# A hybrid decoder step in float32: v and h turned by transposing DMAs instead of TensorE, with h's norm moved into the sigmoid and the weights

## The chip, the cores and the metric

The kernel runs on one core of one Trainium2 chip. The metric is the device time of one execution in microseconds (us). The engines are TensorE (PE in the profile; PEld is its loading of weights), VectorE (DVE), ScalarE (ACT), GpSimd (POOL) and SyncE (SP, which here only queues DMAs). SBUF is the on-chip memory of 128 partitions, PSUM the accumulator memory that PE writes.

## The reference

One layer, 1024 prompt tokens and 8 sample tokens, model width 1024, everything float32. Cut to what matters here:

```
xn = rmsnorm(h, pre_g);  u, v, z_a, x_b, z_b, g_a, g_b = split(xn @ w_in)        # 7 x 1024 columns
vn = layernorm(gelu(v), ln_g, ln_b)                                             # over the 1024 channels of a token
y_a = gelu(u) * (tril(w_s[g]) @ vn + b_s[g]) * silu(z_a)                        # within chunks of 128 tokens, 8 groups
y_b = (pooled(x_b) @ w_pool) * scale * silu(z_b)
m = sigmoid(g_a) * (y_a @ w_pa) + sigmoid(g_b) * (y_b @ w_pb)
h = h + rmsnorm(m @ w_out, post_g)
e = p @ w_ple
gate = sigmoid(rmsnorm(h, ple_in_g) @ w_pg)
h = h + rmsnorm(gate * e, ple_out_g)
```

Outputs are h of both token sets, the normalised v of the last chunk and of the sample, and the pooling buffers.

## The kernel before

**Products.** Every float32 matrix is cut into a high and a low part (`split`: ACT rounds the high part, DVE subtracts it), and a product is three matmuls, high x high, high x low, low x high. The matrices are multiplied by Strassen's scheme with 7 products in place of 8 (`strassen`): a pair of 256 output columns takes 7 steps of 12 or 24 matmuls. A step is named here by the part of the moving operand that it streams: B11, T2, B21, T3, T4, T1, B22, with `x` in front in the profile for the input, `ya`, `yb`, `wo`, `wg` later. Its stationary parts are `vw`, `gaw`, `mw`, `hw` and so on. `evacuate` takes the sums out of PSUM, by ACT for the first product (`u`), mostly by DVE else. PSUM holds three accumulators (`acc`, `acct`) and two small banks.

**Stages, in order of time.** x is normalised and turned (to about 50 us); then v (four pairs, the first without Strassen), g_a, u and z_a, x_b and z_b, g_b, the two merging products, the output product m @ w_out (from about 825 us) and the gate product (to 993 us). Activations lie channels by tokens up to the merge; `big` is one tile of 128 x 8 x 1032 words that holds in turn x, v by tokens, the merged m and the normalised h.

**v.** The v products leave channels by tokens (`v`, one tile for 128 channels), but the layer norm and the mixing need tokens by channels. `v_turn` transposes 128 x 128 blocks on PE into a bank (`vt`), and ACT reads the bank, applies gelu and writes `big`, with the sum of a row as a by-product (`vsums`). The turns of a pair hang on the steps of the next. After the last pair `ln_stats`, `ln_apply`, `v_split` and `spatial` (matmuls `mix`) follow tile by tile in the g_a stage; for the eight sample tokens the same is done in `sv`, and their mixing is the small matmul group `smix`.

**h.** After a pair of 128-token tiles of the output product, `out_finish` normalises it and a DMA queued by POOL adds x. `gate_norm` squares h (ACT), takes the root (POOL, `rstd`) and multiplies (DVE, `hn`); `gate_input` transposes hn on PE into banks (`pht`), and ACT copies these into `big`, times the gain ple_in_g, which is by then one number for each partition. The gate product takes them as `hw`.

**w_pg.** `column_sums` loads w_pg in the x_b and z_b stages (`wgraw`), forms the Strassen sums and stores them in DRAM; the parts B11 and B21 are read from w_pg itself later.

**Order.** Nobody writes the order by hand. `Planner` records every instruction, knows what each reads and writes, estimates its duration, gives it a due time (`late`, and `at` on PE's clock) and then simulates the engines: at each moment it takes, on each engine, the instruction that can start soonest, with ties by due time. The result is a fixed order for each in-order engine. SBUF has 46 slots of equal size (`SLOTS`); an instruction that first writes a slot (`o.fresh`) needs a free one, and a load must leave `SPARE` = 3 free. In the profile all recorded instructions carry the line of `play`, L293, so tiles are told by their names.

Of the kernel before, what the change touches and what calls it, by code (L numbers as in the profile page):

```python
# [10 lines left out]
BF16 = mybir.dt.bfloat16  # L11
AF = mybir.ActivationFunctionType
ALU = mybir.AluOpType

P = 128
# [39 lines left out]
class Planner:  # L55
# [25 lines left out]
    def space(self, ap):  # L81

        dims, start = list(ap.ap), ap.offset
        if "DRAM" in str(ap.space):
            row = ap.tensor.shape[-1]
            first, start = divmod(start, row)
            rows = sum(s // row * (n - 1) for s, n in dims if s >= row)
            return (ap.tensor.name, first, first + rows + 1,
                    ((start, start + sum(s * (n - 1) for s, n in dims if s < row) + 1),))
        row, parts = dims[0]  # L90
        first, start = divmod(start, row)
        pieces = [(start, start + 1)]
# [35 lines left out]
    def duration(self, engine, method, out, reads, kwargs):  # L128
        n = out.free_size()
        if engine == "tensor":  # L130
            return 0.109 if method == "transpose" else max(0.06, 0.0062 + n / 2268)
        if engine == "vector":
            if method == "tensor_reduce":
                n = reads[0].free_size()
            quick = method in ("tensor_scalar", "tensor_scalar_mul", "tensor_copy")
            quick = quick and self.tags.get(reads[0].tensor.name) in (None, "slot")
            return 0.065 + n * (0.00059 if quick else 0.00105) + (0.06 if method[:8] == "scalar_t" else 0)
        if engine == "scalar":
            return max(0.09 + n * 0.00086, 0.26 if n > 1 else 0) + (0.2 if kwargs.get("accum_out") is not None else 0)
        return 0.1 + n * 0.0008 if method == "memset" else 1.0  # L140

    def take(self, engine, method, args, kwargs):
# [14 lines left out]
        if method == "dma_start":  # L157
# [40 lines left out]
    def order(self):  # L198
# [15 lines left out]

        def soonest(o):
            t = max(free[o.engine], o.ready)
            if not o.fixed:
                lead = self.LOAD if o.moved and o.fresh else self.LEAD
                t = max(t, min(o.late - lead, o.at) + slip)
# [14 lines left out]
        while done < len(self.ops):  # L234
            best = None
            for e in self.ENGINES:
# [4 lines left out]
                if could:  # L241
# [7 lines left out]
                    if best is None or now < best[0]:  # L249
                        best = now, o  # L250
            if best is None:
# [48 lines left out]
def hybrid_step(  # L300
# [82 lines left out]
    def root(part, n=P):  # L383

        t, r = sm("ms"), sm("rstd")
# [470 lines left out]
    S = NB  # L856
    xop = Operand("x")
# [7 lines left out]

    def v_turn(out, pair, ts):

        if ts == [S]:
# [3 lines left out]
            places = [(S, ps[:NS, : 2 * P], NS)]  # L872
        else:
# [4 lines left out]
            places = [(t, ps[:, i], P) for i, t in enumerate(ts)]  # L878
        for t, src, n in places:
            nc.scalar.activation(out=vtok(t)[:n, 2 * pair * P : (2 * pair + 2) * P], in_=src,  # L880
                                 func=AF.Gelu_apprx_tanh, accum_out=vsums[:n, t, pair : pair + 1])

    class V(User):
        turns = [[0, 1], [2, 3], [4, 5], [6, 7], [S]]
# [113 lines left out]
    wgcut = {what: dram.tile([HALF, D], F32, tag="wg" + what, name="wg" + what) for what in ('T4', 'B22')}  # L998
    kept["h"] = dram.tile([T, D], F32, tag="h", name="h")
# [262 lines left out]
    for i, u in enumerate(vusers):  # L1262

        nxt = vsteps[1][3:] if i == 0 else (vsteps[i + 1][1:] if i + 1 < NPAIR else gasteps[0][0:])
        if i == 0:
            nxt = vsteps[1][2:]
# [55 lines left out]
    rows = lambda t: NS if t == S else P  # L1322
# [4 lines left out]
    def column_sums(key, src, b):  # L1327
# [25 lines left out]
    column_steps("wg", w_pg, [(bflow[9 + 7 * i], bflow[12 + 7 * i]) for i in range(4)])  # L1353
# [12 lines left out]
    h_of, parts, hn_of, samples = {}, {}, {}, {}  # L1366
# [36 lines left out]

    def gate_norm(t):

        r = rows(t)
        h = h_of.pop(t)
        hn = hn_of[t] = slot("hn", (P, D))
        rs = rstd([square_sum(h[:r], r, scratch=hn)], r)
        nc.vector.tensor_scalar_mul(hn[:r], h[:r], rs[:r])  # L1410

    def gate_input(t):

        hn = hn_of.pop(t)
        if t == S:
            samples["h"] = sample_stationary(hn, NB, gvec[:, 2 * NB :])
# [90 lines left out]
    woop, wgop = stored("wo", w_out, HALF), stored("wg", w_pg, HALF, split=wgcut)  # L1507
# [205 lines left out]
```

## Time and profile before

| | |
|---|---|
| time of 3 runs | 1001.86 us median (1001.23 to 1002.62) |
| the profiled execution | span 1002.0 us from its first to its last instruction, mean granted clock 0.996 |
| busy | PE 989.1, DVE 800.1, ACT 490.0, POOL 73.7 us |
| transposes of v on PE (`vt`) | 64 of 128 x 128 and 8 small ones, from 79.3 to 149.5 us |
| transposes of h on PE (`pht`) | 64, from 858.3 to 935.5 us |
| HBM traffic | 114.59 MB read, 51.77 MB written |

There is no time of the profiled execution beside its span; the span is 0.14 us above the median of the runs. In the rows, `out<-in` names the tile written and the tiles read, `xN` is a count, and a bracket at the end of a row is the idle time of the engine before it and what ended that. A row that gives three durations has the least, the median and the most.

### The profile page before, as it was taken

To read this page: it belongs to the slowest core of one execution; us is meant where nothing else is said; L and a number is where in the kernel's file an instruction comes from. 1 tells how busy PE (TensorE), PEld (TensorE's weight loads), DVE (VectorE), ACT (ScalarE), POOL (GpSimd) and SP (SyncE) were. 2 spreads that over 40 slices of the span, in tenths; PEclk is the share of its full clock that TensorE was granted. 3 is DMA by queue.
4 is the path that set the end of the run, shared out by engine and by line. 5 is a ranking of instruction groups with operands and counts; after the bars stand their busy time and mean duration, and the time that the engine had idled before them with its cause. 6 is when DMAs were issued, how large, how long until landed. Compare 5 with 4: busy or idle time off the path is not lost.

```text
span 1002.0 us, 16159 instructions
## 1 busy us (share of the span) xinstructions
PE 989.1 (99%) x6200; PEld 889.8 (89%) x6200; DVE 800.1 (80%) x1241; ACT 490.0 (49%) x891; POOL 73.7 (7%) x162
## 2 busy tenths in 40 slices
PE   8999999999999999999999999999999999999996
PEld 7889999999999999999999999999999988888885
DVE  5985448877788788788898887697799798779796
ACT  7664356556434343233433343552353365677653
POOL 2200001000000000000000100000000002312111
PEclk9999999999999999999999999999999999999998
DMA  9231214222364345637544166884573553389546
GB/s 353 117 121 43 84 43 129 85 85 86 101 235 169 127 167 183 210 127 252 200 158 143 61 222 244 266 305 148 199 268 107 177 201 71 80 275 364 160 109 188
DMA packets 87330, 166.95 MB, mean 167 GB/s; under 512 B 7614, under 2 KB 47598, under 8 KB 87245
## 3 DMA queue, kind: packets, MB, share of 16 engines
q1 hardware_dynamic: 84885, 158.01, 45.3%
q0 software_dynamic: 2048, 7.37, 4.3%
q8 instruction: 49, 0.80, 0.3%
q10 hardware_dynamic: 320, 0.54, 0.2%
q14 instruction: 28, 0.23, 0.1%
HBM read 114.59 MB, written 51.77 MB: 166 GB/s over the span
## 4 chain that ended last, share of the span: by engine, by line
PE 97%; DVE 1%; POOL 0%; issue 0%; ACT 0%; POOLq 0%; DVEq 0%
PE acc L293 71%; PE acct L293 15%; PE accm L293 2%; PE e L293 2%; PE sps L293 2%; PE mix L293 1%; PE vt L293 1%; PE pst L293 1%; PE pht L293 1%; PE warm L293 1%; DVE sv L293 0%; DVE ge L293 0%; PE smix L293 0%; PE state L293 0%; DVE welo L293 0%
## 5 line engine op out<-in xcount | busy, mean ns | idle before, releaser
L293 DVE TENSOR_TENSOR u<-acc,u 128x520 f32<-128x520 f32 (+1 forms) x90 | 62.5, 695 | 36.5 <-PE acc L293 35.0
L293 POOL TENSOR_TENSOR rstd<-ms,mhalf 128x1 f32<-128x1 f32 (+1 forms) x45 | 38.2, 851 | 204.8 <-DVE ms L293 182.5
L293 POOL MEMSET u<- 128x8 f32 x35 | 3.5, 105 | 556.1 <-PE acc L293 242.5
L293 ACT ACTIVATE u<-acc 128x512 f32<-128x512 f32 x39 | 23.2, 596 | 33.4 <-PE acc L293 33.1
L293 ACT ACTIVATE paw<-pas 128x512 fp32r<-128x512 f32 x16 | 10.0, 627 | 30.0 <-DVE pas L293 24.8
L293 ACT ACTIVATE pbw<-pbs 128x512 fp32r<-128x512 f32 x16 | 10.0, 629 | 29.1 <-DVE pbs L293 25.9
L293 DVE TENSOR_TENSOR big<-big 128x1024 f32<-128x1024 f32 (+4 forms) x20 | 23.6, 1215 | 0.0
L293 ACT ACTIVATE big<-vt 128x256 f32<-128x256 f32 x32 | 11.9, 380 | 21.4 <-PE vt L293 21.4
L293 ACT ACTIVATE big<-pht,gvec 128x128 f32<-128x128 f32 x64 | 18.0, 381 | 8.0 <-PE pht L293 8.0
L293 ACT ACTIVATE big<-mix 128x256 f32<-128x256 f32 x32 | 12.1, 383 | 19.0 <-PE mix L293 18.6
L293 PE MATMUL accm<-qh,wpoolw 128*128 128x260 f32 (+1 forms) x96 | 21.0, 320 | 0.0
L293 ACT ACT_TABLE_LOAD x13 | 16.7, 1283 | 4.6 <-PE acc L293 3.6
L293 DVE TENSOR_TENSOR v<-acc,u 128x520 f32<-128x520 f32 (+1 forms) x9 | 6.3, 697 | 14.9 <-PE acc L293 14.8
L293 DVE TENSOR_TENSOR acc<-acc,u 128x512 f32<-128x512 f32 (+1 forms) x16 | 11.1, 697 | 8.7 <-PE acc L293 8.7
L293 ACT ACTIVATE gbw<-gbs 128x512 fp32r<-128x512 f32 x16 | 10.0, 624 | 16.4 <-DVE gbs L293 13.8
L293 ACT ACTIVATE zaw<-zas 128x512 fp32r<-128x512 f32 x16 | 10.0, 628 | 14.9 <-DVE zas L293 10.6
L293 ACT ACTIVATE zbw<-zbs 128x512 fp32r<-128x512 f32 x16 | 10.1, 630 | 14.6 <-DVE zbs L293 7.3
L293 PEld LDWEIGHTS accm<-qh,wpoolw 128*128 128x128 f32 x96 | 15.5, 188 | 1.9
L293 DVE TENSOR_TENSOR big<-mix,big 128x256 f32<-128x256 f32 x32 | 13.2, 421 | 4.4 <-ACT big L293 3.5
L293 ACT ACTIVATE uw<-us 128x512 fp32r<-128x512 f32 x16 | 9.8, 627 | 13.7 <-DVE us L293 7.2
L293 ACT ACTIVATE zbw<-zbraw 128x512 fp32r<-128x512 f32 x12 | 7.5, 626 | 18.2 <-DMA zbraw<-in_w_in_dram 9.2
L293 ACT ACTIVATE gb<-gb 128x1032 f32<-128x1032 f32 (+1 forms) x8 | 6.8, 854 | 18.8 <-DVE gb L293 18.8
(687 smaller groups left out, 3629.8 us busy)
## 6 DMA issues: line engine op xcount, KB each, us to landing
ga<-ga SPq DMA_DIRECT2D x16, 516.0 KB
gb<-gb SPq DMA_DIRECT2D x16, 516.0 KB
ya<-za SPq DMA_DIRECT2D x8, 516.0 KB
yb<-zb SPq DMA_DIRECT2D x8, 516.0 KB
x<-in_x_prompt_dram SPq DMA_DIRECT2D x8, 512.0 KB
vraw<-in_w_in_dram SPq DMA_DIRECT2D x8, 512.0 KB
e<-e SPq DMA_DIRECT2D x8, 512.0 KB
garaw<-in_w_in_dram SPq DMA_DIRECT2D x8, 512.0 KB
```

The source lines that it names most:

```text
L293: getattr(getattr(self.nc, e), method)(*args, **kwargs)
```

## The change

v and h are no longer turned on PE. A float32 tile is seen as 16-bit words. POOL copies it into a slot with the first words of all its numbers ahead of the second words (`vw`, `hw` as a tile of 16-bit words; `hw` is also the name of the gate product's stationary parts). A transposing DMA on SP's queue turns the sixteen blocks of 128 x 128 words and writes them back over v or h. ACT puts the two halves of each number together again in `big` (`v_join`, and the new `gate_input`). For v, the gelu and its row sum follow as instructions of their own, in place in `big`, by `V.turns` = [7, 0, 1], [2, 3, 4], [5, 6]; the sample's columns are still transposed on PE, now in the first step after the pair.

h is turned raw. Its root goes to `vsums[:, t, :1]` and becomes the scale of the sigmoid (`gated`), so the multiplication on DVE is gone; the gain ple_in_g is multiplied into the rows of w_pg on ACT when `column_sums` loads it, and the left half of the result is stored in a new DRAM tile (`wgleft`), from which B11 and B21 are read. The square of h goes into `big` as a scratch place.

The planner gets durations for the new instructions, and a rule that holds slots back: an instruction that needs a fresh slot is passed over while its time lies more than 3 us beyond PE's, unless nothing else can go (`hard`).

```diff
@@ Planner.duration, Planner.take
-            return max(0.09 + n * 0.00086, 0.26 if n > 1 else 0) + (0.2 if kwargs.get("accum_out") is not None else 0)
+            return max(0.09 + n * (0.00101 if out.dtype == U16 else 0.00086), 0.26 if n > 1 else 0) + (0.2 if kwargs.get("accum_out") is not None else 0)
+        if method == "tensor_copy":
+            return 0.15 + n * 0.0011
...
-            op.busy, op.moved = 1.0 if engine == "gpsimd" else 0.45, writes[0].size() * 4e-6
+            op.busy, op.moved = 1.0 if engine == "gpsimd" else 0.45, writes[0].size() * (2e-6 if writes[0].dtype == U16 else 4e-6)
@@ Planner.order
+                if o.fresh and not hard and t > free["tensor"] + 3.0 and done > 300:
+                    return None
...
-                need = len(o.fresh) + (self.SPARE if o.moved else 0)
+                need = len(o.fresh) + (self.SPARE if o.moved and not hard else 0)
...
+            if best is None and not hard:
+                hard = True
+                continue
+            hard = False
@@ v
+    def v_planes(out, pair):
+        for m in range(2):
+            words, v = slot("vw", (P, 2, SEQ), U16), out[m][:, :SEQ].bitcast(U16)
+            nc.gpsimd.tensor_copy(out=words, in_=v.rearrange("p (t w) -> p w t", w=2))
+            nc.sync.dma_start_transpose(out=v.rearrange("p (k c) -> p k c", c=P),
+                                        in_=words.rearrange("p w t -> p (w t)"))
+    def v_join(out, pair, m):
+        c = 2 * (2 * pair + m) * P
+        nc.scalar.activation(out=big.bitcast(U16)[:, :, c : c + 2 * P].rearrange("p t (c w) -> p t c w", w=2),
+                             in_=out[m][:, :SEQ].bitcast(U16).rearrange("p (w t c) -> p t c w", w=2, c=P), func=AF.Copy)
...
-            ps = bank("vt").rearrange("p (t c) -> p t c", t=2)
-            for i, t in enumerate(ts):
-                for m in range(2):
-                    nc.tensor.transpose(ps[:, i, m * P : (m + 1) * P], out[m][:, t * P : (t + 1) * P], ident)
...
+            nc.scalar.activation(out=v, in_=ps[:NS, : 2 * P] if t == S else v, func=AF.Gelu_apprx_tanh,
+                                 accum_out=vsums[:n, t, pair : pair + 1])
...
-        for s, ts in zip(nxt, V.turns):
-            at(s, lambda u=u, i=i, ts=ts: v_turn(u.out, i, ts))
+        at(nxt[0], lambda u=u, i=i: v_turn(u.out, i, [S]))
+        at(nxt[0], lambda u=u, i=i: v_planes(u.out, i))
+        for m in range(2):
+            at(nxt[2 + m], lambda u=u, i=i, m=m: v_join(u.out, i, m))
+        for s, ts in zip(nxt[4:], V.turns):
+            at(s, lambda i=i, ts=ts: v_turn(None, i, ts))
...
-        s = 3 + 4 * n
+        s = 5 + 4 * n
         at(flow[s], lambda t=t: ln_stats(t))
@@ w_pg and h
+            for i, t in enumerate(raw if cuts else ()):
+                nc.scalar.activation(out=t, in_=t, func=AF.Copy, scale=col(2, 4 * i + b))
+                dma(kept["wgleft"][(4 * i + b) * P : (4 * i + b + 1) * P, :], t[:, :HALF])
...
-        hn = hn_of[t] = slot("hn", (P, D))
-        rs = rstd([square_sum(h[:r], r, scratch=hn)], r)
-        nc.vector.tensor_scalar_mul(hn[:r], h[:r], rs[:r])
+        nc.scalar.activation(out=spare, in_=src, func=AF.Square, scale=D ** -0.5, accum_out=n[:r])
+        root(n, r, rin(t))
+        words = slot("hw", (P, 2, D), U16)
+        nc.gpsimd.tensor_copy(out=words, in_=h.bitcast(U16).rearrange("p (c w) -> p w c", w=2))
+        h_of[t] = h.bitcast(U16).rearrange("p (k t) -> p k t", t=P)
+        nc.sync.dma_start_transpose(out=h_of[t], in_=words.rearrange("p w c -> p (w c)"))
...
-        for k4 in range(0, NB, 4):
-            ps = bank("pht")
-            for k in range(4):
-                nc.tensor.transpose(ps[:, k * P : (k + 1) * P], hn[:, (k4 + k) * P : (k4 + k + 1) * P], ident)
-            for k in range(4):
-                nc.scalar.activation(out=big[:, k4 + k, t * P : (t + 1) * P], in_=ps[:, k * P : (k + 1) * P],
-                                     func=AF.Copy, scale=col(2, k4 + k))
+        nc.scalar.activation(out=words_of(t).rearrange("p k (t w) -> p k t w", w=2),
+                             in_=got.rearrange("p (w k) t -> p k t w", w=2), func=AF.Copy)
...
-        nc.scalar.activation(out=g, in_=src, func=AF.Sigmoid)
+        nc.scalar.activation(out=g, in_=src, func=AF.Sigmoid, scale=rin(t))
```

What this does to the order is seen in three places. First ACT at the end of v, in the first steps of g_a. `vt` are the banks with the last pair's transposes, `sv` the sample's v, `gaw` weight parts, `ga<-acc` an evacuation of g_a, `vh` the squares of the layer norm and the high part for the mixing. Before:

```order
L293 ACTIVATE big,vsums<-vt_359 128x256 x2
L293 ACTIVATE gaw_369<-gas_352 128x512
L293 ACTIVATE big,vsums<-vt_364 128x256 x2
L293 ACTIVATE gaw_380<-garaw_360 128x512
L293 ACT_TABLE_LOAD
L293 ACTIVATE ga_366<-acc_357 128x512
L293 ACT_TABLE_LOAD
L293 ACTIVATE big,vsums<-vt_368 128x256 x2
L293 ACTIVATE big,vsums<-vt_371 128x256 x2
L293 ACTIVATE vh_375,ssq_376<-big,npart_374 128x1024
L293 ACTIVATE sv_109,vsums<-vt_382 8x256
```

The same place after the change, where `v_341` and `v_340` are the second and the first tile of the last pair:

```order
L306 ACTIVATE u_353<-acc_352 128x512
L306 ACTIVATE big,vsums<-big 128x256 x3
L306 ACTIVATE big<-v_341 128x8x256
L306 ACTIVATE sv_109,vsums<-vt_354 8x256
L306 ACTIVATE gaw_364<-gas_348 128x512
L306 ACTIVATE vh_371,ssq_372<-sv_109,npart_370 8x1024
L306 ACTIVATE big<-v_340 128x8x256
L306 ACT_TABLE_LOAD
L306 ACTIVATE ga_362<-acc_352 128x512
L306 ACT_TABLE_LOAD
L306 ACTIVATE big,vsums<-big 128x256 x4
```

The two joins (`big<-v`) now stand ahead of the sample's gelu and of the evacuation of g_a, and the last pair's gelus come behind both.

Second, PE at `smix`. Before, with the g_a product's step B22 ahead of it and T2 behind:

```order
L293 MATMUL acc_394<-xB22l_232,gaw_369 128x260 x2
L293 MATMUL acc_394<-xB22h_231,gaw_369 128x260 x2
L293 MATMUL smix_396<-diag,sv_109 128x8 x8
L293 MATMUL acc_414<-xT2h_244,gaw_391 128x260 x2
L293 MATMUL acc_414<-xT2l_245,gaw_391 128x260 x2
```

After, `rowsum` being two matmuls for the offsets of the mixing:

```order
L306 MATMUL acc_367<-xT4l_279,gaw_359 128x512
L306 MATMUL acc_367<-xT4h_278,gaw_359 128x512
L306 MATMUL rowsum_399<-wst_290,ones_397 128x512 x2
L306 MATMUL smix_389<-diag,sv_109 128x8 x8
L306 MATMUL acc_378<-xT1h_261,gaw_361 128x260 x2
L306 MATMUL acc_378<-xT1l_262,gaw_361 128x260 x2
```

smix has moved forward by three steps, from behind B22 to between T4 and T1 of the first pair of g_a. The steps from the last pair's T1 to it are now B11 of g_a, B22 of v, then T2, B21, T3 and T4 of g_a, with the sample's two transposes between T2 and B21.

Third, SP in the gate stage, after the change, with `h_1358` and `h_1366` the tiles of the third pair:

```order
L306 DMA wgB22l_1449<-wgB_125 128x2x512
L306 DMA wgB22h_1450<-wgB_125 128x2x512
L306 DMA h<-h_1358 128x1024
L306 DMA h<-h_1366 128x1024
L306 DMA wgB22l_1451<-wgB_125 128x2x512
L306 DMA_TRANSPOSE h_1358<-hw_1397 128x16x128
L306 DMA_TRANSPOSE h_1366<-hw_1394 128x16x128
L306 DMA out_1423<-in_ple_out_g_dram 128x1024
```

Before, the store of the first of these tiles stood ahead of twelve weight loads and the other behind six of them; now both stores, and the transposes that follow them, stand behind the run of weight loads, and nothing is left between the two transposes.

More of the change, by code (lines that the diff above doesn't have):

```diff
@@ L81, in space @@
     def space(self, ap):
-        dims, start = list(ap.ap), ap.offset
+        size = 2 if ap.dtype in (BF16, U16) else 4
+        dims, start = [(s * size, n) for s, n in ap.ap], ap.offset * size
         if "DRAM" in str(ap.space):
-            row = ap.tensor.shape[-1]
+            row = ap.tensor.shape[-1] * size
             first, start = divmod(start, row)
@@ L88, in space @@
             return (ap.tensor.name, first, first + rows + 1,
-                    ((start, start + sum(s * (n - 1) for s, n in dims if s < row) + 1),))
+                    ((start, start + sum(s * (n - 1) for s, n in dims if s < row) + size),))
         row, parts = dims[0]
         first, start = divmod(start, row)
-        pieces = [(start, start + 1)]
+        pieces = [(start, start + size)]
         for s, n in reversed(dims[1:]):
@@ L218, in soonest @@
                 lead = self.LOAD if o.moved and o.fresh else self.LEAD
-                t = max(t, min(o.late - lead, o.at) + slip)
+                term = min(o.late - lead, o.at)
+                t = max(t, term + slip)
+                if o.fresh and not hard and t > free["tensor"] + 3.0 and done > 300:
+                    return None
             if o.moved and len(rings[o.engine]) >= 8:
@@ L381, in rstd, with root @@
         return r
-    def root(part, n=P):
-        t, r = sm("ms"), sm("rstd")
+    def root(part, n=P, r=None):
+        t, r = sm("ms"), sm("rstd") if r is None else r
         nc.vector.tensor_scalar(out=t[:n], in0=part[:n], scalar1=EPS, scalar2=None, op0=ALU.add)
@@ L856, in hybrid_step @@
     S = NB
+    rows = lambda t: NS if t == S else P
     xop = Operand("x")
@@ L1352, in hybrid_step @@
     bflow = [s for x, z, _ in bsteps for p in (x, z) for s in p]
-    column_steps("wg", w_pg, [(bflow[9 + 7 * i], bflow[12 + 7 * i]) for i in range(4)])
+    column_steps("wg", w_pg, [(bflow[8 + 7 * i], bflow[11 + 7 * i]) for i in range(4)])
     def sample_product(st, op):
@@ L1506, in hybrid_step @@
     FIRST = ("P1", "P7", "P6", "P2", "P4", "P5", "P3")
-    woop, wgop = stored("wo", w_out, HALF), stored("wg", w_pg, HALF, split=wgcut)
+    woop, wgop = stored("wo", w_out, HALF), stored("wg", kept["wgleft"], HALF, split=wgcut)
     outsteps = [strassen(Turned(i, "m"), woop, Out(i), Tokens, None if i else FIRST) for i in range(NPAIR)]
```

36 lines of the change are left out of this document (20 added, 16 removed).

## The prediction

> **What bounds the kernel now.** I read the page first: the busy shares, the chain of waits, and the strip of 40 slices.
>
> ```profile
> PE 989.1 (99%) x6200; PEld 889.8 (89%) x6200; DVE 800.1 (80%) x1241; ACT 490.0 (49%) x891; POOL 73.7 (7%) x162
> ACT  7664356556434343233433343552353365677653
> PE 97%; DVE 1%; POOL 0%; issue 0%; ACT 0%; POOLq 0%; DVEq 0%
> ```
>
> PE is the chain: 97% of the span belongs to it, and it is idle for 1002.0 - 989.1 = 12.9 us in all. The list of waits says that between start and tail nothing but one wait of 0.2 us stops it:
>
> ```profile
> PE warm L293 <- POOL ident masks.py:199: 1.9, 1, 1.9
> PE e L293 <- ACT wehi L293: 1.2, 1, 1.2
> PE e L293 <- DVE welo L293: 0.8, 1, 0.8
> PE smix L293 <- DVE sv L293: 0.2, 1, 0.2
> ```
>
> So an instruction taken off PE shortens the run by what it occupies there, and an addition elsewhere costs something only when PE comes to wait for it. Next I read the busy time by stretch, the v stage first and then the output and gate stages (columns: width, PE, PEld, DVE, ACT, POOL, granted clock, DMA share, GB/s).
>
> ```profile
> 75.00:100.00 25.00, 25.00 (x177) 22.99 (x176) 14.51 (x24) 12.06 (x38) 0.00 (x0) 1.00 0.14 43
> 100.00:125.00 25.00, 25.00 (x176) 23.25 (x175) 11.91 (x18) 9.81 (x33) 0.00 (x0) 1.00 0.25 85
> 900.00:925.00 25.00, 25.00 (x119) 20.52 (x117) 22.96 (x33) 18.55 (x43) 5.36 (x5) 1.00 1.05 364
> 950.00:975.00 25.00, 25.00 (x110) 20.27 (x109) 24.03 (x41) 13.68 (x30) 4.05 (x5) 1.00 0.44 105
> sum 125.00, PE 125.00 PEld 102.12 DVE 103.48 ACT 85.66 POOL 27.38; mean PE 25.00 PEld 20.42 DVE 20.70 ACT 17.13 POOL 5.48
> ```
>
> The last row sums 850 to 975. In the v stage DVE and ACT are half idle; in the gate stage DVE has 125 - 103.5 = 21.5 us to spare in 125, and as little as 1 to 2 us in two of the stretches.
>
> **What leaves PE.** The view by tile counts the transposes; three rows of the timeline give their price.
>
> ```profile
> L293 PE MATMUL vt<-ident,v x72: 270/272/329, 79.3 to 149.5; 128*128 128x128 f32 x64, 128*8 128x128 f32 x8
> L293 PE MATMUL pht<-ident,hn x64: 270/272/299, 858.3 to 935.5; 128*128 128x128 f32 x64
> 861.95 0.39 PE L293 MATMUL acct<-woB22h,mw 128*128 128x512 f32 x1
> 864.72 1.03 PE L293 MATMUL pht<-ident,hn 128*128 128x128 f32 x8
> 865.51 0.48 PE L293 MATMUL acct<-woT2h,mw 128*128 128x512 f32 x1
> ```
>
> The 272 ns are the latency of one, not what it occupies: eight of them start at 864.72 and the next product at 865.51, so one takes 0.79 / 8 = 0.099 us. The eight transposes of the sample's v stay. 64 + 64 go: 128 x 0.099 = 12.6 us. A step of twelve products runs from 861.95 to 864.72, 2.77 us; I use it below as PE's clock.
>
> **What comes in their place.** Each of 16 blocks (8 of v, 8 of h) now passes POOL (a copy of 128 x 2048 words), SP (one transposing DMA of 512 KB) and ACT (a join of 128 x 2048 words). No row shows such an operation, so each is bounded.
>
> ```profile
> L293 POOL TENSOR_SCALAR_AFFINE_SELECT ws<-ws 128x1024 f32<-128x1024 f32 x1 | 1.7, 1725 | 25.4 <-DMA ws<-in_w_s_dram 25.4
> L293 POOL MEMSET mst<- 128x1024 f32 x1 | 1.0, 955 | 31.1 <-PE acc L293 31.1
> L293 ACT ACTIVATE hn<-h x8: 1043/1060/1102, 847.0 to 930.6; 128x1024 f32<-128x1024 f32 x8
> L293 DVE TENSOR_SCALAR hn<-h,rstd x8: 733/747/755, 850.8 to 933.8; 128x1024 f32<-128x1024 f32 x8
> 858.93 2.18 ACT L293 ACTIVATE big<-pht,gvec 128x128 f32<-128x128 f32 x8 [0.32 <-PE pht L293]
> DMA to landing us min/median/max: 5.5/6.3/10.0
> q1 hardware_dynamic: 84885, 158.01, 45.3%
> L293 SPq DMA_DIRECT2D wgraw<-in_w_pg_dram x8: 404/495/1109, 421.4 to 494.5; - x8
> ```
>
> POOL copy: by elements, twice the memset or twice the select, 1.9 to 3.45 us; I take the middle, 2.7, since a copy reads as the select does but tests nothing. Join on ACT: 1.06 us by bytes, 2.1 by elements; I take 2.1, the row being one element per lane and step. Transposing DMA: 512 KB at the 364 GB/s of the busiest stretch would be 1.4 us; the 512 KB transfers that POOL queues (x added to h, h to the result) land in 5.5 to 10.0, the row above; cut into rows of 128 words, 256 bytes, it is 2048 pieces, and a piece of q1 takes 0.453 x 16 x 1002 / 84885 = 85.6 ns of one engine, so 2048 x 85.6 / 16 = 11.0 us on sixteen. I take 5.5: nearest in size, and the lowest of its row because nothing is added here and POOL writes no descriptors. The Trainium skill, page "DMA: Bandwidth & Descriptors", section "Latency and other measured facts", has 261 GB/s for a transposing DMA with a strided middle dimension; an estimate from that is 2.0 us, by which the wait worked out next would vanish and the sum be 989.4. No run here shows it yet.
>
> In v, ACT keeps its gelus and gains eight joins, 8 x 2.1 = 17 us spread over some 70 of which it was half idle. In the gate stage it loses 8 x 2.18 = 17.4 us of copies out of PSUM and gains 8 x 2.1 = 16.8: nothing. DVE loses eight normalisations, 8 x 0.747 = 6.0 us, and the sample's. The scaling of w_pg's rows is eight ACT instructions of 1.06 us and eight stores, from 421 us, the first load, to some 20 us past the last at 494.5, where ACT's strip stands at 2 to 4 tenths; that idle time hides them, and without it they would cost 8.5 us. The root as the sigmoid's scale adds no instruction. Slots held back alter the order in which loads are queued, on SP above all; where PE's order changes outside the two stages it is two exchanges of neighbouring steps, for which I put nothing.
>
> **Where the longer path shows.** Behind a join on ACT, in order, stand weight splits and evacuations, and in one place the sample's last gelu. PE's only wait hung there already:
>
> ```profile
> 149.79 0.37 ACT L293 ACTIVATE sv<-vt 8x256 f32<-8x256 f32 x1 [0.81 <-PE vt L293]
> 158.42 1.92 PE L293 MATMUL smix<-diag,sv 8*128 8x8 f32 x16 [0.15 <-DVE sv L293]
> 160.00:165.00 5.00, 5.00 (x29) 4.94 (x29) 2.73 (x6) 2.21 (x3) 1.47 (x1) 0.66 0.87 313
> ```
>
> From that gelu to smix is 8.6 us. In the changed order the sample's gelu stands behind the join of the last pair's second tile. That tile is complete when step T1 of the last pair is evacuated (1.0 us with hand-over), then copy 2.7, DMA 5.5, join 2.1, and 8.6 to smix: 19.9 us. PE meanwhile runs B11, B22, T2, B21, T3 and T4, two sample transposes and two row sums: 6 x 2.77 + 0.2 + 0.5 = 17.3. It waits 2.6, where it waited 0.15: +2.4. With the DMA at 1.4 the chain is 15.8 and nothing waits; at 10.0 it is 24.4 and 7.1 wait. The granted clock fell to 0.66 for 5 us behind the thin work at smix, which loses 5 x 0.34 = 1.7 us; it may vanish or come twice, so +/-1.7, and 0 in the sum. The mixing of the tiles begins six steps after smix and has some 3 us of air by the same count.
>
> **Sum.** The span of the profiled execution is 1002.0, 0.1 above the median of the runs: 1002.0 - 12.6 + 2.4 = **991.8 us**. Its own range: 1002.0 - 12.6 - 0.15 - 1.7 = 987.5 to 1002.0 - 12.6 + 7.0 + 1.7 = 998.1.
>
> **Rivals.** *The transposes land late and ACT is held* (slower). At 11.0 us, the last pair costs 25.4 - 17.3 = 8.1, and 1.7 for the clock. In each of the seven other pairs ACT meets the first join four steps (11.1 us) after the tile is complete and the data at 1.0 + 2.7 + 11.0 = 14.7; the second lands 11.0 later, at 25.7, while ACT, after a join and three splits of 0.63 (the size of the split in the row below), stands there at 18.7: held for 7.0.
>
> ```profile
> L293 ACT ACTIVATE vw<-vraw 128x512 fp32r<-128x512 f32 x13 | 8.0, 629 | 3.5 <-PE acc L293 3.5
> ```
>
> Three accumulators let PE run two steps, 5.5, ahead; it waits 1.5 and loses 1.7 of clock, 3.2 x 7 = 22.4. In all 1002.0 - 12.6 + 32.2 = 1021.6. Between 5.5 us (a loss of 2.4) and 11.0 (32.2) the gain is eaten at 7.4 us a transpose: the point that decides. For it: the only comparable landings scatter up to 10.0, and 900 to 925 runs the DMA at a share of 1.05. Against: the v stage runs it at 0.14 to 0.25. The Trainium skill, page "VectorE: DVE Perf Modes", section "The three transpose paths", gives 1309 ns for one 128 x 128 block by DMA; sixteen in series would be 20.9 us, an estimate deep inside this rival; no run here shows whether they run in series.
>
> *POOL shuts DVE out in the gate stage* (still faster). These rows show the two engines in each other's way:
>
> ```profile
> 848.66 2.14 POOL L293 TENSOR_TENSOR rstd<-ms,mhalf 128x1 f32<-128x1 f32 x1 [3.03 <-DVE ms L293]
> 862.12 0.56 POOL L293 TENSOR_TENSOR rstd<-ms,mhalf 128x1 f32<-128x1 f32 x1 [2.73 <-DVE ms L293]
> 849.10 0.67 DVE L293 TENSOR_TENSOR mw<-big,mw 128x512 fp32r<-128x512 f32 x1
> 849.70 0.67 DVE L293 TENSOR_TENSOR ms<-ms,big 128x512 f32<-128x512 f32 x1
> ```
>
> The same instruction takes 0.56 us beside an idle DVE and 2.14 beside one that reads two tiles back to back. Turned round, eight copies of h at 3.45 block DVE for 27.6 us; it has 21.5 - 6.3 (this stage's half of PE's saving) + 6.0 = 21.2 free. The 6.4 left over reach PE: 991.8 + 6.4 = 998.2. Against: in the rows POOL is the one that waits, and at 2.7 the copies (21.6) about fit. The Trainium skill, page "SBUF — State Buffer", section "Who interferes with whom", says that a DVE instruction with two SBUF inputs and a GpSimd one that reads SBUF exclude each other for a whole instruction, whichever began first; by that rule the block on DVE is as real as the one the rows show on POOL.
>
> *The DMA moves single words.* 262,144 pieces at 85.6 / 16 ns are 1.4 ms each: over 20 ms in all. Then it would not be a block transpose at all; the destination of whole 128 x 16 x 128 blocks speaks against it.
>
> **How the numbers follow.** Runs spread over 1.4 us, so 0.2% (2 us) is about what can be told from no change. Forecast 0.53; DVE shut out 0.12; between them and late landing, within 2 us of 1001.9, 0.05; late landing 0.27; single words 0.03. Faster 0.65, same 0.05, slower 0.30. The range runs from 987, the forecast's low end, to 1016, a landing of 10.0 us on the line above, where the comparable row ends: it leaves out half of the late case, the single words and a little below, 0.18.
>
> **What would show it.** Right: vt only x8 and pht gone, PE busy near 976 us, PE's waits headed by smix with under 8 us, DMA to landing of the transposes under 7.4. Wrong: ACT waiting on v or h DMAs for more than 7 us a pair and PE on acc weights behind it; or DVE beyond 24 of 25 in the gate stage and its 0.67 us instructions stretched beside POOL copies; or copies above 3.45 us.

## The result, and the profile after

The changed kernel takes 1010.09 us in the median of 5 executions (1004.83 to 1011.20), the kernel before, beside it, 1001.86 (1001.23 to 1003.82): a ratio of 1.0069, 95% interval 1.0045 to 1.0092. It is 0.7% slower; 991.8 was forecast. The profiled execution is the shortest of the five, 1004.83 us with a span of 1003.1.

The page first: busy times, all DMA packets, SP's queue (q1) and POOL's (q0).

```profile
PE 978.6 (98%) x6072; PEld 876.5 (87%) x6072; DVE 803.3 (80%) x1231; ACT 516.8 (52%) x851; POOL 104.9 (10%) x178
DMA packets 121760, 177.41 MB, mean 177 GB/s; under 512 B 41022, under 2 KB 81006, under 8 KB 121677
q1 hardware_dynamic: 119317, 168.50, 49.9%
q0 software_dynamic: 2048, 7.37, 4.2%
```

PE does 10.5 us less than the 989.1 before (12.6 were summed), and the span is longer all the same: PE stands idle for 24.5 us instead of 12.9. q1 has 34,432 more packets, the sixteen transposing DMAs at 2048 pieces each and little else. Its share went from 45.3% of 1002.0 to 49.9% of 1003.1 us on 16 engines, 746 us more, which is 22 ns a piece.

The groups of the page and the views by tile (least, median and most nanoseconds of a row, then the time from issue to landing, of `vw` and of `hw`) give what the new steps cost; two rows of the timeline (start, duration) follow.

```profile
L306 POOL COPY vw<-v 128x2048 uint16<-128x2048 uint16 x8 | 16.6, 2076 | 62.8 <-DVE vw L306 30.8
L306 ACT ACTIVATE big<-v 128x2048 uint16<-128x2048 uint16 x8 | 17.2, 2151 | 8.5 <-DMA v<-vw 8.5
L306 ACT ACTIVATE big<-h 128x1024 f32<-128x1024 f32 (+1 forms) x16 | 25.7, 1608 | 14.8 <-DMA h<-hw 12.4
L306 SPq DMA_TRANSPOSE v<-vw x8: 1566/2483/5376, 70.4 to 133.6; - x8
DMA to landing us min/median/max: 4.4/6.6/8.9
L306 SPq DMA_TRANSPOSE h<-hw x8: 1647/2414/6046, 849.5 to 948.8; - x8
DMA to landing us min/median/max: 4.5/4.5/4.5
941.05 3.60 SPq L306 DMA_TRANSPOSE h<-hw  x1
946.76 2.17 ACT L306 ACTIVATE big<-h 128x2048 uint16<-128x2048 uint16 x1 [7.69 <-DMA h<-hw]
```

The copy (2.08 us) and the join (2.15) are as forecast. A transposing DMA occupies SP itself for 1.6 to 6 us, where the other DMAs on SP's queue take 0.4 us in the median (0.3 to 3.3). The trace tells the landing of three of the sixteen: 4.4 and 8.9 us after the issue in v, 4.5 in h. ACT waits 8.5 us for v's and 12.4 for h's; the longest of these waits, 7.69 us, ends at 946.76, for a transposition that SP issued at 941.05, so it was issued late rather than slow to land.

Now PE: its list of waits (total, times, longest), and the gate stage by stretch (width, PE, PEld, DVE, ACT, POOL, granted clock, DMA share, GB/s).

```profile
PE acct L306 <- DVE ge L306: 3.9, 3, 1.9
PE acct L306 <- DVE h L306: 2.1, 1, 2.1
PE acc L306 <- ACT big L306: 2.1, 1, 2.1
PE acct L306 <- ACT hw L306: 1.5, 1, 1.5
PE acct L306 <- ACT u L306: 1.3, 1, 1.3
875.00:900.00 25.00, 22.86 (x99) 18.32 (x98) 16.46 (x22) 17.02 (x25) 9.84 (x8) 1.00 1.05 313
925.00:950.00 25.00, 23.15 (x99) 18.14 (x97) 14.35 (x22) 14.26 (x20) 8.88 (x9) 1.00 0.94 243
950.00:975.00 25.00, 21.31 (x89) 16.44 (x90) 21.85 (x38) 18.32 (x33) 4.25 (x4) 1.00 0.43 110
```

In these three stretches PE had 25.00 of 25 before; now it lacks 2.1, 1.9 and 3.7 us, with VectorE far from full in the second (14.35 of 25). The one of these waits that lies outside the output and gate stages (`acc <- ACT big`) stands at the start of g_a. smix, where the prediction put the wait, has none.

### The profile page after: what moved, and what is told of

Read it like the earlier page. It is cut to its first block, busy times and chain, and to the rows that moved or that the text cites. A ratio compares the mean times of both kernels' runs of the same rounds, so it can differ in the third digit from the quotient of the medians.

```text
span 1003.1 us, 15896 instructions
## 1 busy us (share of the span) xinstructions
PE 978.6 (98%) x6072; PEld 876.5 (87%) x6072; DVE 803.3 (80%) x1231; ACT 516.8 (52%) x851; POOL 104.9 (10%) x178
## 3 DMA queue, kind: packets, MB, share of 16 engines
q1 hardware_dynamic: 119317, 168.50, 49.9%
q0 software_dynamic: 2048, 7.37, 4.2%
## 5 line engine op out<-in xcount | busy, mean ns | idle before, releaser
L306 POOL TENSOR_TENSOR rstd<-ms,mhalf 128x1 f32<-128x1 f32 (+1 forms) x36 | 29.2, 813 | 176.4 <-DVE ms L306 176.4
L306 ACT ACTIVATE big<-h 128x1024 f32<-128x1024 f32 (+1 forms) x16 | 25.7, 1608 | 14.8 <-DMA h<-hw 12.4
L306 ACT ACTIVATE pbw<-pbs 128x512 fp32r<-128x512 f32 x16 | 10.0, 629 | 27.7 <-DVE pbs L306 24.5
L306 POOL COPY vw<-v 128x2048 uint16<-128x2048 uint16 x8 | 16.6, 2076 | 62.8 <-DVE vw L306 30.8
L306 ACT ACTIVATE big<-v 128x2048 uint16<-128x2048 uint16 x8 | 17.2, 2151 | 8.5 <-DMA v<-vw 8.5
L306 PE MATMUL accm<-qh,wpoolw 128*128 128x260 f32 (+1 forms) x96 | 20.9, 319 | 0.0
L306 POOL COPY hw<-h 128x2048 uint16<-128x2048 uint16 x8 | 16.4, 2049 | 16.1 <-DMA h<-in_x_prompt_dram 8.2
L306 DVE TENSOR_TENSOR big<-mix,big 128x256 f32<-128x256 f32 x32 | 12.9, 421 | 4.7 <-ACT big L306 3.9
L306 DVE TENSOR_TENSOR xb<-acc,u 128x520 f32<-128x520 f32 (+1 forms) x12 | 8.3, 695 | 10.4 <-PE acc L306 10.2
```

The source lines that it names most:

```text
L306: getattr(getattr(self.nc, e), method)(*args, **kwargs)
```

## The experiments

Three theories at first. **A**: the loss is in the gate stage, where a transposing DMA stands on SP behind weight loads and holds ACT, which runs in order. **B**: the planner's hold-back rule displaces loads everywhere. **C**: POOL's copies shut VectorE out. Ratios are to the kernel before, run beside each (1002.4 to 1003.1 us), with 95% intervals.

### The change in halves

`v_half`: `gate_norm`, `gate_input`, `gated` and `column_sums` as in the kernel before, the rest as changed.

> The v half of the change alone: v turned by transposing DMAs, h with its norm and its PE transposes as before, the planner's new rule kept. Theory A (the loss sits in the gate stage, where a transposing DMA stands on SP behind weight loads and the next join holds ACT): the v half keeps what the trace of after shows at the start of x_b, 3 to 5 us of gain, so 997 to 999 us, with one wait of some 2 us of PE in the first steps of g_a. Theory B (the planner's hold-back rule displaces loads everywhere): 1003 or more, with PE waits outside the two stages. Theory C (GpSimd's copies shut VectorE out, which counts only where VectorE is nearly full): 997 to 999 as well, since VectorE is half idle here.

`h_half`: `v_turn` and its steps as before, the rest as changed.

> The h half alone: raw h turned by DMAs, root in the sigmoid, gain in w_pg's rows; v turned on PE as before; the planner's new rule kept. Theory A: the gate stage loses what it loses in after, 1.5 to 8 us net, so 1003 to 1010, with PE waiting on wg parts and ge behind an ACT that waits for h<-hw. Theory B: also slow, but with waits spread over all stages. Theory C: 1003 to 1010 too, and in the gate stage VectorE, not ACT, is what PE's waits go back to, with the VectorE rows beside POOL's copies stretched.

`hold_rule`: the kernel before, and (shortened to the condition; `hard` and its uses come with it)

```
+                if o.fresh and not hard and t > free["tensor"] + 3.0 and done > 300:
+                    return None
```

> The kernel before with the planner's hold-back rule alone (an instruction that needs a fresh slot is passed over while its time lies over 3 us beyond PE's); nothing of v, h or w_pg changed. Theory A: 1001 to 1003, no change. Theory B: 1004 to 1010. Theory C says nothing of it: 1001 to 1003.

Measured: v half 1000.06 us, ratio 0.9976 (0.9966 to 0.9985); h half 1018.81, 1.0155 (1.0124 to 1.0185); rule alone 1003.17, 1.0001 (0.9991 to 1.0010). B is out. The v half gains 2.4 us, a little less than expected, and all of the loss is the h half's; alone it is even larger than in the changed kernel, and larger than A or C had it.

The h half's profile shows an event that the profiled execution of the changed kernel does not have so plainly. PE's longest wait, ACT's timeline (in brackets its idle time and what ended it), the stretches, and then the DMA view of 890 to 900 us:

```profile
PE acct L306 <- ACT wgB21h L306: 15.5, 1, 15.5
904.87 2.15 ACT L306 ACTIVATE big<-h 128x2048 uint16<-128x2048 uint16 x1 [14.62 <-DMA h<-hw]
890.00:895.00 5.00, 5.00 (x23) 4.10 (x22) 2.68 (x4) 0.25 (x2) 0.89 (x1) 1.00 1.27 115
895.00:900.00 5.00, 2.73 (x13) 1.91 (x11) 0.69 (x1) 0.00 (x0) 0.00 (x0) 1.00 1.49 67
q1 hardware_dynamic: 1583, 0.44, 85.6%
q0 software_dynamic: 126, 0.47, 52.3%
```

The join that ends this wait starts 20.4 us after the issue of its transposition (884.45). The view counts the DMA engines as busy for more than the whole of the time, at 1.27 and 1.49, and they move 115 and 67 GB/s; the kernel before moves 263 and 306 in these two stretches. POOL's pieces (x added to h, 4 KB each) take 0.523 x 16 x 10 us / 126 = 664 ns; over the changed kernel's whole run they take 0.042 x 16 x 1003 / 2048 = 329. q1's pieces, nearly all of a transposition, take 87 ns instead of 22. So **theory D**: a transposing and an adding DMA in flight together slow each other, and everything queued behind them.

### Room in the order

`sp_price`: the changed kernel, with the transposing DMA at the trace's price in the planner.

```
+            if method == "dma_start_transpose":
+                op.busy, op.lands = 2.5, 2.7
```

> The changed kernel with one line more in the planner: a transposing DMA is priced at 2.5 us of SP and 6.6 us to landing (the medians of after's trace) in place of 0.45 and 3.9. Its order puts the fourth tile's transposition ahead of six weight loads and three of the transpositions closer to their copies; the joins move later in ACT's order. Theory A: ACT's waits for h<-hw shrink and the time falls to between 994 and 1003. Theory C: the copies still exclude VectorE, so no more than 2 us are won: 1006 to 1010. Theory B: no change, 1008 to 1011.

1012.44 us, 1.0098 (1.0075 to 1.0121): no gain, where A forecast one, and just above the ranges of B and C. Its profile has the same event, 103 and 92 GB/s from 890 to 900, though the transposes now stand closer to their copies.

### The suspect brought into the v stage

`v_accum` and `v_plain`: the v half with one DMA more on POOL's queue per transposition, and a tile for it. The two differ in the last argument alone, and their order is the same. (Two lines that set the planner's order and landing for this DMA are left out here.)

```
+            other = slot("other", (P, D))
+            nc.gpsimd.memset(other, 0.0)
             nc.gpsimd.tensor_copy(out=words, ...)
             nc.sync.dma_start_transpose(...)
+            nc.gpsimd.dma_start(out=other, in_=x_prompt[...], accum_op=ALU.add)   # v_plain: without accum_op
```

> The v half alone, and beside each of its eight transposing DMAs a DMA of 512 KB that POOL queues and that adds x to a spare tile nobody reads. Theory D (new, from the h half, where from 890 to 905 us a transposing and an adding DMA were in flight together and moved 67 to 128 GB/s at a full share of the DMA engines): the two slow each other, so transposes that overlap an adding DMA land in 10 us or more, ACT is held at the joins and PE waits: 1004 to 1020 us. Theory A (only the place in SP's queue counts): the v stage has bandwidth to spare, 999 to 1002 as the v half without it.

> The control: the same kernel in the same order, but POOL's eight extra DMAs copy x into the spare tile and add nothing. Theory D: 999 to 1002, transposes landing in 4 to 9 us as in the v half alone. If it is not the addition but any second queue or the bytes, this one slows like the other: 1004 to 1020.

1024.47 (1.0213; 1.0196 to 1.0231) and 1017.92 (1.0145; 1.0130 to 1.0159). The control is slow as well, so it is none. The view by tile shows where, and PE's longest wait in each:

```profile
L306 SPq DMA_TRANSPOSE v<-vw x8: 1567/2752/7506, 69.1 to 149.6; - x8
PE smix L306 <- DVE sv L306: 9.4, 1, 9.4
```

```profile
L306 SPq DMA_TRANSPOSE v<-vw x8: 1526/4102/7713, 71.0 to 153.5; - x8
PE smix L306 <- DVE sv L306: 10.4, 1, 10.4
```

The first is `v_plain`, the second `v_accum`. In both the last transposition is late, at 149.6 and 153.5 instead of 133.7 us, and smix waits. POOL makes the extra tiles of the last pair early (129.0 and 130.5 us in `v_plain`) and then stands idle for 13.7 us, put down to VectorE's `gaw`, before that pair's copies; that they wait for a slot is likely and was not taken apart. It is the chain that the prediction had priced, lengthened. The flag costs 6.5 us more in the same order, and `v_accum` is slower than D had it. But adding pieces take twice as long as copied ones where no transposition is in flight (302 and 142 ns from 130 to 140 us), so this pair does not decide on D. It shows a limit of D, though: from 155 to 163 us in `v_accum` pieces of both kinds are in flight, and 157 GB/s move at a share of 1.12, beside 198 from 151 to 157 us in `v_plain`. How far the rate falls when the two meet is not the same each time, and what decides it was not found.

### The suspect taken out of the gate stage

`x_by_dve`: the changed kernel, with

```
-        nc.gpsimd.dma_start(out=h, in_=x_of(t), accum_op=ALU.add)
+        xa = slot("xadd", (P, D))[:r]
+        dma(xa, x_of(t))
+        add(h, h, xa)
```

> The changed kernel with x added to h by VectorE (a plain load of x on SP, then one addition of 128 x 1024 a tile, some 1.2 us each by the rows of that kind) in place of the adding DMA on POOL's queue. Six adding DMAs remain at the end of the gate stage. Theory D: the collapse between 885 and 905 us is gone, 996 to 1003 us and less scatter between runs. Theory A: the weight loads still stand ahead on SP, 1006 to 1011. Theory C (POOL's copies against VectorE): 10 us more on VectorE make it worse, 1010 to 1016.

1001.19 us, 0.9985 (0.9973 to 0.9997), in the middle of D's range and far from A's and C's. (The loads of x are now on SP's queue, and the planner made the order anew.) The stretch of the event now reads

```profile
890.00:895.00 5.00, 5.00 (x23) 4.06 (x22) 5.00 (x6) 4.66 (x7) 3.23 (x2) 1.00 1.03 403
895.00:900.00 5.00, 5.00 (x23) 3.91 (x22) 5.00 (x6) 4.71 (x8) 0.00 (x0) 1.00 1.04 384
```

`h_copied`: the h half, `accum_op` dropped, so that x is copied over h and the sum is left out; every engine's order is unchanged.

> The h half (1018.8) with one flag changed and its order the same instruction for instruction: the DMA that POOL queues after the output product copies x over h and adds nothing. It leaves out the addition (h becomes x), so only its time counts. Theory D (adding and transposing DMAs slow each other): 1000 to 1006, no stretch of 15 us with 60 to 130 GB/s. Theory E (POOL's queue and SP's queue disturb each other whatever they carry, as the control in the v stage suggests): 1012 to 1022.

1006.63 us, 1.0037 (1.0011 to 1.0063): 11.8 us less than the h half through one flag. It is just above D's range, well below E's. Here the transposition is nearly over when POOL's pieces come, at 889; the ten microseconds from 890 hold little of it (152 pieces under 512 bytes) and move 359 GB/s. What there is of a meeting, from 889.5 to 890.5 us:

```profile
889.50:890.50 1.00, 1.00 (x6) 0.83 (x5) 1.00 (x1) 0.46 (x2) 0.00 (x0) 1.00 1.41 88
```

So the rate falls beside a copying DMA too, for 1 us; in `v_plain` it is 63 GB/s from 154.0 to 155.5. E as forecast, a kernel as slow without the flag, is out. That a copying DMA disturbs nothing is not shown, and how much of the 11.8 us is the meeting, its moment, or the longer time of adding pieces, this pair does not tell.

### The square: adding and transposing, each with and without

`no_turn` (on `x_by_dve`) and `no_turn_adding` (on the changed kernel) leave out the turning of h:

```
-        h_of[t] = h.bitcast(U16).rearrange("p (k t) -> p k t", t=P)
-        nc.sync.dma_start_transpose(out=h_of[t], in_=words.rearrange("p w c -> p (w c)"))
+        h_of[t] = words.rearrange("p w (k t) -> p (w k) t", t=P)
```

> x added by VectorE as in the kernel with 1001.2, and h's eight transposing DMAs taken out: the join reads POOL's copy directly. It leaves out the turning of h. Theory A (what is left of the loss in the gate stage is the transposing DMA, its time on SP behind weight loads and its landing): 994 to 997, that is the v half's 1000 less 6.3 for PE's transposes. Theory C (POOL's copies and their exclusion of VectorE): 1000 to 1002, no change.

> The changed kernel with h's transposing DMAs taken out and the adding DMAs kept: the fourth corner beside the changed kernel (both, 1010), x by VectorE (transposing alone, 1001) and that without the turning (neither, 997). It leaves out the turning of h. Theory D (it is the two together): 995 to 999, the adding DMAs cost nothing by themselves. If the adding DMAs are slow by themselves and h is late for that: 1003 to 1007, and the square adds up without an interaction.

| ratio | x added by DMA | x added by VectorE |
|---|---|---|
| h turned by DMA | 1.0069 (1.0045 to 1.0092), again 1.0055 (1.0037 to 1.0074) | 0.9985 (0.9973 to 0.9997) |
| not turned | 0.9983 (0.9974 to 0.9991), 1000.82 us | 0.9944 (0.9929 to 0.9960), 997.22 us |

C falls: without the transposes, and with all of POOL's copies, the stage gains (997 where C had 1000 to 1002). The transposing DMA costs 4.1 us where VectorE adds x. Adding by DMA costs 3.9 us even without it, which I had not expected (1000.82 lies between both ranges). Together they cost another 3.8 us: the mean of the two upper left ratios and the lower right one, less the other two corners. Its interval, from the half-widths added as squares, is about 2.6 either way. So D holds for a part only: some 4 us are the two together, 4 each of them alone. The planner made a new order for each corner, so a part of each figure may be the order's; in the gate stage `h_half` and `h_copied` alone have one order. Why adding by DMA costs 4 us without a transposition beside it was not taken apart. No run has the kernel before with x added by VectorE, so it is open whether that kernel pays them too.

### Where the longer executions come from

> The changed kernel once more, unaltered: the profile of its first execution was of the shortest of five (1004.8 beside 1009.6 to 1011.2) and shows no collapse of the DMA. Theory D: a profile of a longer execution shows, between 885 and 910 us or 940 and 960, a stretch of some 10 us with adding and transposing DMAs at under 150 GB/s and a share of the engines of 1.2 or more, and a wait of PE of 5 us or more behind it; if this one is short again (1005 or less), it shows none. Against D: a long execution without such a stretch.

The changed kernel once more: 1008.65 us in the median, the profiled execution 1008.25. PE's longest wait, ACT's timeline, and three stretches:

```profile
PE acct L306 <- ACT wgB21h L306: 6.9, 1, 6.9
893.60 2.16 ACT L306 ACTIVATE big<-h 128x2048 uint16<-128x2048 uint16 x1 [6.05 <-DMA h<-hw]
885.00:890.00 5.00, 5.00 (x23) 4.07 (x22) 2.81 (x5) 0.69 (x2) 1.45 (x2) 1.00 1.34 185
895.00:900.00 5.00, 0.10 (x1) 0.00 (x0) 2.78 (x2) 5.00 (x7) 2.42 (x2) 0.99 1.03 343
900.00:905.00 5.00, 2.98 (x7) 2.43 (x8) 5.00 (x6) 5.00 (x8) 0.20 (x1) 0.50 1.05 392
```

The event is here, shorter than D had it and, over 5 us, not under its 150 GB/s: a share of 1.34 and 185. From 887 to 891 it is 113 GB/s, where the shortest execution moves 289. In that one the same 5 us read

```profile
885.00:890.00 5.00, 5.00 (x23) 4.05 (x22) 2.81 (x5) 0.69 (x2) 1.45 (x2) 1.00 1.15 263
```

In the longer one ACT is held for 6.05 us, its casts of gate weights come late, PE stands for 6.9 and then runs at half clock for a stretch. This one wait covers the 3.4 us between the two spans (1006.5 and 1003.1), and more. It is one longer execution beside one short one.

### What of the change is worth keeping

`h_raw_on_pe`: the v half, and raw h with the root in the sigmoid and the gain in w_pg, but turned on PE. (Shortened; ACT copies four blocks out of PSUM with one instruction.)

```
-        words = slot("hw", (P, 2, D), U16)   # copy, transposing DMA and join
+        nc.tensor.transpose(ps[:, k * P : (k + 1) * P], got[:, (k4 + k) * P : (k4 + k + 1) * P], ident)
```

> The v half, and of the h half only the algebra: raw h, root as the sigmoid's scale, gain in w_pg's rows, but h turned on PE into banks as before (64 transposes). If the algebra is free, as the prediction had it: 998 to 1001, the time of the v half. If the eight stores of w_pg's left half or the root's new place cost something: 1002 or more.

1001.77 us, 0.9982 (0.9972 to 0.9993): within the interval of the v half. The algebra costs nothing that can be told, and gains nothing.

`three_pairs`: the v half, with the last pair of v turned on PE as before.

```
+        if i == NPAIR - 1:
+            for s, ts in zip(gasteps[0], [[0, 1], [2, 3], [4, 5], [6, 7], [S]]):
+                at(s, lambda u=u, i=i, ts=ts: v_turn_pe(u.out, i, ts))
+            continue
```

> The v half with the last pair of v turned on PE as before and three pairs by DMA; h as before. The wait at the start of g_a came from the last pair alone. Theory A: 48 transposes of 0.099 us leave PE, 4.8 us, and nothing waits: 997 to 999 beside 1002 to 1003 for the kernel before, better than the v half. If the joins cost something in each pair: 1000 or more.

997.42 us, 0.9950 (0.9938 to 0.9962): 5.0 us for 48 transposes, where 4.8 were worked out. No pair but the last costs anything that can be told.

`x_by_dve_sp_price`: `x_by_dve` and `sp_price` together.

> x added by VectorE, and the planner prices a transposing DMA at 2.5 us of SP and 6.6 us to landing. Theory A: with the collapse gone, room for the transposes in the order now pays: 996 to 1000. Theory C: 1000 to 1003, no change.

1018.01 us, 1.0163 (1.0139 to 1.0187), a plain miss of both theories (A and C). The planner's answer to a dearer transposition was to bring the last pair's later: the last of them is issued at 962.8, beside the adding DMAs with which the gate stage ends, and ACT waits 8.17 us for it. A truer price gave no better order in `sp_price` and a worse one here.

`three_and_first_h`: three pairs of v and the first pair of h by DMA, the rest on PE. Shown for `gate_norm`; `gate_input` turns these tiles as in `h_raw_on_pe`:

```
+        if t > 1:
+            return
         words = slot("hw", (P, 2, D), U16)
```

> A version built from what the runs left standing: v by DMA in three pairs and on PE in the last, raw h with the root in the sigmoid, h by DMA for the first pair of tiles alone (at 845 to 855 us, where no weights are loaded and no adding DMA is in flight), on PE for the other three. Theory A and D: 16 transposes more leave PE, 1.6 us: 995 to 997, at or a little below the three pairs' 997.4. If the first pair's join or the algebra costs something: 997.5 to 1000.

996.29 us, 0.9945 (0.9931 to 0.9959). This and `three_pairs` beat both kernels; they can't be told from each other.

## Why the prediction was wrong

**What held.** The 0.099 us of a PE transpose (5.0 us for 48). Copy 2.08 for 2.7, join 2.15 for 2.1. The landings that the trace tells, 4.4, 4.5 and 8.9 for 5.5, inside the bounds. The algebra at nothing. The v stage too: it was forecast at 6.3 - 2.4 = 3.9 us of gain, and the v half gained 2.4, with the wait in another place and, by the trace, not for the reason given: that the wait came within 0.5 us of the 2.6 worked out for smix is luck. The timeline (SP, ACT, VectorE and PE of the changed kernel) and the clock, and last the same wait of PE in `after_again`:

```profile
132.03 0.93 SPq L306 DMA_DIRECT2D garaw<-in_w_in_dram  x2
133.60 5.38 SPq L306 DMA_TRANSPOSE v<-vw  x1
142.56 2.15 ACT L306 ACTIVATE big<-v 128x2048 uint16<-128x2048 uint16 x1 [5.04 <-DMA v<-vw]
146.06 0.60 ACT L306 ACTIVATE ga<-acc 128x512 f32<-128x512 f32 x1
151.09 0.69 DVE L306 TENSOR_TENSOR ga<-acc,u 128x520 f32<-128x520 f32 x1
151.93 0.49 PE L306 MATMUL acc<-xB22h,gaw 128*128 128x260 f32 x2 [2.08 <-ACT big L306]
150.00:155.00 5.00, 3.07 (x15) 3.10 (x16) 4.90 (x18) 1.91 (x8) 0.00 (x0) 0.73 0.00 0
PE acc L306 <- DVE ga L306: 2.1, 1, 2.1
```

The last pair's join holds ACT for 5.04 us, but PE passes smix at 142.87 without a wait. It stops 7 us later, and the two profiles of one and the same order put this down once to ACT's `big` and once to VectorE's evacuation, which ends at 151.78, 0.15 us before PE goes on; in VectorE's order steps of the mixing stand ahead of it. So a wait in the new order is shown, and that the landing causes it is not. With the last pair on PE (`three_pairs`) it is gone.

The v half's sum by the trace is 2.1 us of wait, and a second stretch of low clock behind the one at 0.66 that the kernel before has too, 5 x 0.27 = 1.4: 6.3 - 3.5 = 2.8, where 2.4 were measured.

**The step that failed** is one sentence under "What comes in their place": "In the gate stage it loses 8 x 2.18 = 17.4 us of copies out of PSUM and gains 8 x 2.1 = 16.8: nothing." It counts ACT's busy time, and the joins came out as said (2.15 us). It leaves out when the eight joins can start, in the stage that had the full DMA, and a join that cannot start holds ACT, which runs in order. The late landing was priced as a rival for all eight pairs, but with one landing time everywhere; in v, at a share of 0.14 to 0.25 before the change, PE stops once, and the row of 900 to 925 us with 1.05 was quoted "for it" and given no price of its own. What the runs show instead, with x added by DMA as in the kernel before: with h's 64 transposes off PE and copies and joins in their place, but no transposing DMA, nothing is gained that can be told (0.9982 of `h_raw_on_pe` to 0.9983 of `no_turn_adding`, each to 0.001) where 6.3 us were summed, and the transposing DMAs cost another 7.9 us (to 1.0062, the mean of 1.0055 and 1.0069). With x on VectorE it is a gain of 3.8 (`no_turn`, 0.9944) and a cost of 4.1. What kept these gains from 6.3 was not taken apart.

**The rivals.** The late landing came true in sign and in its mechanism (ACT held, casts late, PE on its weights), in h above all, and not by its price: 11.0 us rested on 85.6 ns a piece, and a piece takes 22; the time goes into late issue, SP's own time and the meeting with other DMAs. The prediction's own sign of it is there in the last pair of h, where ACT waits 7.69 and 1.72 us. The Trainium skill, page "DMA: Bandwidth & Descriptors", section "Latency and other measured facts", gave 261 GB/s, an estimate of 2.0 us; the engines' own time here is 2048 x 22 / 16 ns = 2.8 us, not far off, but 4.4 is the least landing in the changed kernel and 3.7 in `sp_price`. The Trainium skill, page "VectorE: DVE Perf Modes", section "The three transpose paths", has 1309 ns for one block; sixteen in series, an estimate of 20.9 us, are not what the traces show where the DMA is quiet, with landings of 4.4 and 8.9 us in v. VectorE shut out does occur (VectorE twice, then the copy on POOL):

```profile
895.21 1.22 DVE L306 TENSOR_TENSOR wgB11l<-wgB,wgB11h 128x1024 fp32r<-128x1024 f32 x1
897.55 4.05 DVE L306 TENSOR_TENSOR wgT2l<-wgT,wgT2h 128x1024 fp32r<-128x1024 f32 x2
897.00 2.38 POOL L306 COPY hw<-h 128x2048 uint16<-128x2048 uint16 x1 [3.84 <-DMA h<-in_x_prompt_dram]
```

Two such instructions take 4.05 us beside the copy. But `no_turn`, with all copies, gains, so this is not what makes the loss.

**The basis.** Span and time were set equal. An execution is 1.7 us longer than its span (1004.83 and 1003.1), so the sum, made on a span, was 1.7 us low as a time of that execution. By the same 1.7 the profiled execution of the kernel before took some 1003.7 us, an estimate, 1.8 above the median; so against the median the sum was not low. The two cancel by luck.

## What to carry to other kernels

Price a moved step in each stage it moves to, and by the resource that is full there: here a DMA in place of PE work paid in the stage that had a DMA share of 0.14 to 0.25 and lost in the one that had up to 1.05, and the busy time of the engine that waits for it said nothing of that. Look at what else is in flight when it lands: beside adding DMAs the transposing ones cost 7.9 us, without h's adding DMAs 4.1. Where the work can be split, put on the DMA the part that falls into a quiet stretch: three of four pairs of v gave 5.0 us, all four 2.4, v and h together a loss.

## What was not expected of the hardware

- With transposing and adding DMAs in flight together, sixteen engines moved 67 GB/s at a share of 1.49 for 5 us in `h_half`; from 155 to 163 us in `v_accum` they moved 157. Beside copying DMAs the rate fell as well, for 1 to 1.5 us (88 GB/s in `h_copied`, 63 in `v_plain`). Why was not found. The Trainium skill, page "DMA: Bandwidth & Descriptors", section "SWDGE vs HWDGE vs iDMA", says that an engine takes turns between its queues; no run here shows whether that bears on it.
- A transposing DMA of 512 KB keeps SP for 1.5 to 7.7 us (7.7 in `v_accum`, 7.4 with x by VectorE, behind weight loads), and whatever is queued on SP next stands behind it.
- An adding DMA's piece of 4 KB took 302 ns in `v_accum` where a copied one took 142 in `v_plain` (130 to 140 us); in the changed kernel's whole run POOL's adding pieces take 329.
